# Output projection: a fifth pair by seven products in its first half, a pinned copy in the fold, and an add moved into the last matmul group

## The chip, the cores and the metric

The kernel runs on one core of one Trainium2 chip. The metric is device time in microseconds (us) of one execution, the median of several runs. Everything is one program of five engines that run side by side: PE (TensorE, matmuls; its weight loads are shown as PEld), DVE (VectorE), ACT (ScalarE), POOL (GpSimd) and SP (SyncE, which here only issues transfers), beside 16 DMA engines.

## The reference

One decoder block of width 2048 on 256 tokens, all in float32:

```python
proj = x @ w_in                       # columns: GLA q,k,v,gate,low rank; FoX q,k,v,f; two merge gates
y_gla = gla(...) @ w_branch_gla       # gated linear attention
y_fox = fox(...) @ w_branch_fox       # softmax attention with a forget bias
merged = sigmoid(ma) * y_gla + sigmoid(mb) * y_fox
x = layer_norm(ALPHA * x + merged @ w_out)
h = gelu(causal_dwconv(x @ w_gate)) * (x @ w_up)
x = layer_norm(ALPHA * x + h @ w_down)
x = x + sigmoid(x @ w_ple_gate) * (p @ w_ple_proj)
```

The change sits in `merged @ w_out` (the output projection, 256 x 2048 by 2048 x 2048), in the step that adds its partial sums into the residual, and at the very end of the last line.

## The kernel before

**Numbers as sums of two.** Matmuls run on a rounded format. Each float32 operand is split into a high part (a copy on ACT, line 121, tiles `hi`, `hi_b`, `hi_t`) and a low part (a subtraction on DVE, lines 215 and 241, tiles `lo`, `lo_b`, `lo_t`), and each product is three matmuls: high by high, high by low, low by high.

**Units.** All weights come from one array `wu` of 1 MB units, loaded by SP in program order (its schedule is written by hand, line 123), split by ACT and DVE, and used by PE. `unit(ahead=3)` (line 249) hands PE unit u and first prepares all up to u+2. Weights as loaded stand in the ring `raw` (5 buffers of half a unit), the split ones in `rhi` and `rlo` (6 buffers of half a unit each). The pool `big` (tag S8) has 15 buffers of 1 MB for all else that is large.

**Pairs and two ways to multiply them.** A projection with width 2048 runs in two halves of 1024 columns (`s_half`, line 818, `nh` 0 and 1). A unit holds the weights of one pair of 128 rows, as four 128 x 512 blocks: one pair by two column blocks; the activations of a pair are 2 x 2 blocks too (two row blocks by two token blocks). `classic` (line 844) does the eight block products, 24 matmuls of 128 x 512. `strassen` (line 852) does seven products of sums, 21 matmuls, whose results add up in seven PSUM accumulators. It needs sums of activation blocks (`mS`, made by `sums`, line 800) and differences of weight blocks (line 157). Which pairs go which way is in `WO_S`: pairs 1, 2, 3, 5 of the first half, 1, 3, 5 of the second. `OUT_ORDER` is the order of the pairs: 0, 1, 3, 4, 5, 2, 6, 7, and 0, 1, 3, 5, 2, 4, 6, 7. The output projection is units 120 to 135.

**Stored differences.** For the pairs in `WO_T` the weight differences are not made when they are needed but earlier, during the branch projections (units 96 to 119, the loop at line 1154): `park_gen` (line 174) loads a unit into an S8 buffer (line 178), lets two units of PE pass, makes the differences in place (four DVE operations of 128 x 512, line 159) and stores it with POOL's queue (line 172); each unit takes three of the 24 steps `pull(1, parks)` of that stage, so seven units take 21. When the pair's turn comes, `prep_s` (line 185) loads blocks b11 and b22, b21 from `wu` (lines 193 and 194; 0.25 and 0.5 MB) and the stored unit (line 196; 1 MB, into one more S8 buffer), and splits three and a half half-units instead of two.

**Activations.** `turn_pair` (line 1131) transposes one pair of the merged activations during the branch stage, pairs 6 and 7 in `begin_out` (line 1385) after the first unit. A pair in `WO_C` (0, 4, 6, 7) is split as it is into `mC`, two pairs to an S8 buffer; any other goes through `sums` into an S8 buffer of its own.

**Fold.** After the last seven-product pair of a half, `fold` (line 862) adds the accumulators p1, p5, p6, p7 into the residual tiles: one copy of p1 to SBUF on ACT (line 873) and eight DVE operations. DVE and ACT instructions are put in order when the program is built, by priority and by a simulation; `keep_in_program_order(i)` pins an instruction behind everything traced before it on its engine. Here the first DVE operation of the fold is pinned in first halves; the copy is not. `fold` serves four halves with a residual: two of the output projection and two of the down projection. The next half takes the accumulators' PSUM banks over.

**The end.** The last accumulator of the last half is made in two 256-column halves (line 906). For each, `ev_g` (line 1614) adds it on DVE to what is already summed in `zg` (line 1623), and `put` (line 1575) does tanh on ACT, two DVE operations and a store by SP.

Of the kernel before, what the change touches and what calls it, by code (L numbers as in the profile page):

```python
# [14 lines left out]
ALU = mybir.AluOpType  # L15
# [25 lines left out]
P_STAT = 5000  # L41
# [11 lines left out]
GR_T = ((1, 2, 5, 7), (1, 2, 5, 7))  # L53
GR_S = ((1, 2, 4, 5, 7),) * 2
X_S = (1, 2, 4, 5, 7)
WO_S = ((1, 2, 3, 5), (1, 3, 5))
WO_C = (0, 4, 6, 7)

DN_ORDER = (tuple(range(NF // 2)),
            tuple(range(NF // 2)))  # L60
DN_S = ((1, 3, 5, 6, 8, 9, 11, 12, 14, 15, 17, 18), (1, 3, 5, 6, 8, 9, 11, 12, 14, 15))


WO_T = ((1, 2, 3, 5), (1, 3, 5))
DN_T = ((3, 6, 9, 12, 15, 18), (3, 6, 9, 12, 15))
PG_ORDER = (tuple(range(8)), tuple(range(8)))
PG_S = ((), (2, 3, 4))
# [11 lines left out]
def tile_block(ctx: ExitStack, tc: tile.TileContext, wu, wfv, wpp, xT_in, x_in, pT_in, wlr,  # L79
               chan, gnorm, lng, ident_in, mask_in, cmask_in, out):  # L80
    nc = tc.nc
# [38 lines left out]
    def copy(o, i, scale=1.0):  # L120
        return nc.scalar.activation(o, i, AF.Copy, bias=0.0, scale=scale)  # L121
# [8 lines left out]
    for _ in range(8):  # L130
# [7 lines left out]
               for b, order, sset in ((52, GV_ORDER, GV_S), (68, GV_ORDER, GR_S),  # L138
                                      (120, OUT_ORDER, WO_S), (dn0, DN_ORDER, DN_S),
                                      (NU - 16, PG_ORDER, PG_S))  # L140
# [133 lines left out]
    ident = cst.tile([P, P], F32, name="ident")  # L274
# [183 lines left out]
    for u in range(8):  # L458
        hi, lo = fvu[u]
        for j in range(2):  # L460
# [8 lines left out]
            for t, i, c in seq:  # L469
# [3 lines left out]
                                 start=kt == 0 and i == 0, stop=kt == 15 and i == 2)  # L473
# [178 lines left out]
    for n in range(16):  # L652
        h, j = n // 2, n % 2
        hi, lo = unit()

        ps = (mxtile if n == 0 else mmtile)(f"psf{'qk'[j]}{h}")
# [112 lines left out]
    for n in range(16):  # L769
        nm, dst, sc = (("q", gq, 1.0 / 16.0), ("k", gk, 1.0))[n // 2 % 2]  # L770
        h, c = n // 4, n % 2
        hi, lo = unit()
        ps = mmtile(f"ps{nm}{2 * h + c}")
# [44 lines left out]
    def s_half(nm, nh, order, sset, cl, st, zof, ev, tail=0, mid={}, end=None, ahead=3,  # L818
               residual=True, fine=None):

        if nh == 0:
            C = [[mmtile(f"{nm}0_{t}{c}") for c in range(2)] for t in range(2)]
            p1, p5 = [mmtile(f"{nm}0_p{i}") for i in (1, 5)]
            p6 = p7 = None
        else:
            C = [[f(f"{nm}1_{t}{c}") for c in range(2)] for t, f in enumerate((mxtile, mmtile))]
            p1, p5, p6, p7 = [mmtile(f"{nm}1_p{i}") for i in (1, 5, 6, 7)]  # L830
        left = (0, 1, 6, 3, 5, 4, 2)
        n, ns = len(order), len(sset)
        total = {id(C[t][c]): 6 * (n - ns) + 3 * ns * (t * c == 0) for t in range(2)
                 for c in range(2)}
        if fine:
            total[id(C[1][1])] -= 6 * tail
        done = {}

        def mm(ps, x, w, e=slice(0, 512)):
            k = done[id(ps)] = done.get(id(ps), 0) + 1  # L840
            nc.tensor.matmul(ps[:, e], lhsT=x, rhs=w, start=k == 1,  # L841
                             stop=k == total.get(id(ps), 3 * ns))

        def classic(pair, w, toks=(0, 1), cs=(0, 1)):
            for j in range(2):
                for t in toks:
                    ah, al = cl(pair, j, t)
                    for x, v in ((ah, w[0][j]), (ah, w[1][j]), (al, w[0][j])):
                        for c in cs:
                            mm(C[t][c], x, v[:, c * 512:c * 512 + 512])  # L850

        def strassen(pair, ops):
            nonlocal p6, p7
            if p6 is None:
                p6, p7 = [mxtile(f"{nm}0_p{i}") for i in (6, 7)]
            prods = (p1, C[0][0], C[0][1], p5, p7, p6, C[1][0])
            for ps, i, (hi, lo) in zip(prods, left, ops):
                ah, al = st(pair, i)
                for x, v in ((ah, hi), (ah, lo), (al, hi)):
                    mm(ps, x, v)  # L860

        def fold():
            g0, g1 = 2 * nh, 2 * nh + 1
            u = t2("fold")
            axpy = lambda z, p: nc.vector.scalar_tensor_tensor(z, z, ALPHA, p, ALU.mult, ALU.add)
            add = lambda z, p: nc.vector.tensor_tensor(z, z, p, ALU.add)
            if not residual:
                copy(zof(0, g0), p1)
                for o, x, p in ((u, zof(0, g0), p6), (zof(0, g1), u, p5), (zof(1, g0), u, p7),
                                (zof(1, g1), zof(1, g0), p5)):  # L870
                    nc.vector.tensor_tensor(o, x, p, ALU.add)
                return
            copy(u, p1)
            i = axpy(zof(0, g0), p1)
            if nh == 0:
                tc.keep_in_program_order(i)
            add(u, p6)
            axpy(zof(0, g1), u)
            add(zof(0, g1), p5)
            add(u, p7)  # L880
            axpy(zof(1, g0), u)
            add(u, p5)
            axpy(zof(1, g1), u)

        for i, pair in enumerate(order[:n - tail]):
            (strassen if pair in sset else classic)(pair, unit())
            if i in mid:
                mid[i]()
            if pair in sset and not set(order[i + 1:]) & set(sset):
                fold()  # L890
        us = [unit(ahead) for _ in range(tail)]

        def tail_mm(t, c, i):
            classic(order[n - tail + i], us[i], (t,), (c,))
            if i == tail - 1:
                ev(t, c, C[t][c])

        if fine:
            fine(C[1][1])
            for t, c in ((0, 0), (0, 1), (1, 0)):  # L900
                for i in range(tail):
                    tail_mm(t, c, i)
            last = [(x, v[:, 512:1024]) for i in range(tail) for j in range(2)
                    for ah, al in (cl(order[n - tail + i], j, 1),)
                    for x, v in ((ah, us[i][0][j]), (ah, us[i][1][j]), (al, us[i][0][j]))]
            halves = [mmtile(f"{nm}{nh}_11{b}")[:, 0:256] for b in "bc"]
            for b, ps in enumerate(halves):
                for k, (x, v) in enumerate(last):
                    nc.tensor.matmul(ps, lhsT=x, rhs=v[:, 256 * b:256 * b + 256], start=k == 0,
                                     stop=k == len(last) - 1)  # L910
            ev(1, 1, None, halves)
            return
        if tail:
            end(tail_mm)
            return
        for t in range(2):
            for c in range(2):
                ev(t, c, C[t][c])
# [212 lines left out]
    def turn_pair(pair):  # L1131
# [7 lines left out]
        p3 = pt.rearrange("p (k t) -> p k t", t=S)  # L1139
        if pair not in WO_C:  # L1140
            yp = t2("yp")
            copy(yp, pt)
            mS[pair] = sums(yp.rearrange("p (k t) -> p k t", t=S), f"mS{pair}", 0.5,
                            pair not in WO_S[1])
            return
        i = WO_C.index(pair)
        if i % 2 == 0:
# [84 lines left out]
    def out_proj(nh, tail, mid, end=None):  # L1232
        def cl(pair, j, t):
            if pair not in WO_C:
                return cell(mS[pair], ((0, 7), (1, 2))[j][t])
            i = WO_C.index(pair)
            a = mC[i // 2][:, i % 2 * 2 + j, :]
            return a[:, t * P:t * P + P], a[:, 256 + t * P:256 + t * P + P]

        def ev(t, c, ps):  # L1240
            zc = z1of(t, 2 * nh + c)
            with tc.high_priority(P_STAT):
# [3 lines left out]

        s_half("wo", nh, OUT_ORDER[nh], WO_S[nh], cl, lambda pair, i: cell(mS[pair], i), z1of, ev,
               tail, mid, end)
# [160 lines left out]
    for n in range(NF):  # L1409
# [18 lines left out]
        u = t1("up")  # L1428
# [4 lines left out]
        if pair in DN_S[0]:  # L1433
            if j == 0:
                yp = t2("yp").rearrange("p (k t) -> p k t", t=S)
            h = yp[:, j, :]
        else:
            h = y
# [4 lines left out]
        if pair in DN_S[0] and j == 1:  # L1443
            v = s_sums(yp)
            for i in range(2):
# [4 lines left out]
                k = DN_S[0].index(pair)  # L1450
# [124 lines left out]
    def put(z, nh, t, c, ab=(0, 512)):  # L1575
        th = t2("tho")
        r = t2("res")
        e = slice(*ab)
        w = slice(c * 512 + ab[0], c * 512 + ab[1])
        o = slice(nh * 1024 + w.start, nh * 1024 + w.stop)  # L1580
        nc.scalar.activation(th[:, e], z, AF.Tanh, bias=0.0, scale=0.5)
        nc.vector.scalar_tensor_tensor(th[:, e], th[:, e], 1.0, pp[nh][:, t, w],
                                       ALU.add, ALU.mult)
        nc.vector.scalar_tensor_tensor(r[:, e], th[:, e], 0.5, z2[nh][:, t, w],
                                       ALU.mult, ALU.add)
        (nc.gpsimd if nh == 0 else nc.sync).dma_start(out[t, :, o], r[:, e])
# [27 lines left out]
    def ev_g(t, c, ps, halves=None):  # L1614
        z = zg[:, t, c, :]
        if halves is None:
            nc.vector.tensor_tensor(z, z, ps, ALU.add)
            put(z, 1, t, c)
            return
        for b, h in enumerate(halves):  # L1620
            e = slice(256 * b, 256 * b + 256)
            with tc.high_priority(P_STAT):
                nc.vector.tensor_tensor(z[:, e], z[:, e], h, ALU.add)
            put(z[:, e], 1, t, c, (e.start, e.stop))

    def pre_g(ps):
        z = zg[:, 1, 1, :]
# [61 lines left out]
def _layout(i):  # L1689
# [9 lines left out]
         _sst(c("gv", 2048), GV_ORDER, GV_S), _sst(c("gr", 2048), GV_ORDER, GR_S), m[PSM1:]] + br  # L1699
        + [_sst(i["w_out"][0], OUT_ORDER, WO_S), gu,  # L1700
           _sst(i["w_down"][0], DN_ORDER, DN_S),
# [44 lines left out]
```

## Time and profile before

| | |
|---|---|
| three runs | 1648.08, 1648.25, 1648.61 us; median 1648.25 |
| profiled execution, its own time | 1648.3 us |
| its span, first instruction to last | 1646.5 us |
| granted TensorE clock | 1.00 |
| busy: PE, PEld, DVE, ACT, POOL | 1639.6, 1405.6, 1339.6, 904.5, 89.5 us |
| DMA | 460.23 MB, mean 280 GB/s |

The profiled execution is one run; 1.8 us of its time lie outside the span (1648.3 less 1646.5). In rows of a timeline the columns are start, duration, engine, line, operation, tiles written and read, and the count of merged instructions; in brackets is the idle time ahead of it and what ended it. Durations of matmuls overlap their successors, so the pace of PE is read from the starts. Rows of stretches give start and end, length, then busy time and count of each engine, the granted clock, the DMA engines' busy share and GB/s. A wait is who waited, for whom, us in total, times, longest.

### The profile page before, as it was taken

The page shows a single profiled execution, that of the slowest core. Times are in us where ns is not written, and L with a number is a line of the kernel's source. Part 1 is how long each engine was busy: PE and PEld are TensorE (multiplying, and loading weights), DVE is VectorE, ACT ScalarE, POOL GpSimd, SP SyncE. Part 2 cuts the span into 40 slices and gives each one's busy share as a digit, 9 for nine tenths or more (in the row PEclk, how much of TensorE's full clock was granted, in tenths as well). Part 3 has the DMA queues.
Part 4 walks back from the last instruction along what each step waited for, and adds up shares of the span by engine and source line. Part 5 has one row for each costly group of instructions (what it writes and reads, how often), then busy time and mean ns, then how long its engine had stood idle before and what let it go on. Part 6 is the DMA issues. An engine that isn't in the chain of part 4 may idle for free.

```text
span 1646.5 us, 23416 instructions
## 1 busy us (share of the span) xinstructions
PE 1639.6 (100%) x8432; PEld 1405.6 (85%) x8432; DVE 1339.6 (81%) x1926; ACT 904.5 (55%) x1261; POOL 89.5 (5%) x238
## 2 busy tenths in 40 slices
PE   9999999999999999999999999999999999999998
PEld 8988888888888888888898888888888888888887
DVE  7677789898889767777987888887877778989787
ACT  6655545456666654446574444555555456566554
POOL 0000000000000000000010111110111000000000
PEclk9999999999999999999999999999999999999999
DMA  8777689977887658888855898888766679899574
GB/s 323 279 261 278 230 322 344 373 269 281 298 292 268 227 197 309 306 309 316 299 191 190 314 341 319 302 306 306 282 237 216 210 260 339 306 353 340 169 260 157
DMA packets 112100, 460.23 MB, mean 280 GB/s; under 512 B 12728, under 2 KB 14016, under 8 KB 94704
## 3 DMA queue, kind: packets, MB, share of 16 engines
q1 hardware_dynamic: 103344, 406.30, 69.3%
q0 software_dynamic: 8640, 52.44, 8.1%
q8 instruction: 66, 1.08, 0.3%
q14 instruction: 50, 0.41, 0.1%
HBM read 406.25 MB, written 52.44 MB: 279 GB/s over the span
## 4 chain that ended last, share of the span: by engine, by line
PE 98%; DMA 1%; DVE 0%; ACT 0%; issue 0%; POOL 0%; SPq 0%; DVEq 0%; ACTq 0%; POOLq 0%
PE psm L973 11%; PE dn L841 10%; PE psu L307 10%; PE psg L307 9%; PE psa L973 5%; PE psu L309 5%; PE psg L309 5%; PE dn_p L841 4%; PE gv L841 3%; PE gr L841 3%; PE wo L841 3%; PE pg L353 3%; PE psb L973 3%; PE fv L472 2%; PE psk L307 2%; PE psq L307 2%
## 5 line engine op out<-in xcount | busy, mean ns | idle before, releaser
L241 DVE TENSOR_TENSOR lo<-raw,hi 128x1024 fp32r<-128x1024 f32 x464 | 561.4, 1220 | 165.9 <-ACT hi L121 163.9
L121 ACT ACTIVATE hi<-raw 128x1024 fp32r<-128x1024 f32 x464 | 486.5, 1058 | 342.8 <-issue 66.2
L307 PE MATMUL psu<-x1T,hi 128*128 128x512 f32 x688 | 240.4, 392 | 0.0
L307 PE MATMUL psg<-x1T,hi 128*128 128x512 f32 x672 | 234.8, 392 | 0.0
L309 PE MATMUL psu<-x1T,lo 128*128 128x256 f32 x688 | 192.3, 280 | 0.0
L309 PE MATMUL psg<-x1T,lo 128*128 128x256 f32 x672 | 187.8, 280 | 0.0
L973 PE MATMUL psm<-hi,xT 128*128 128x512 f32 x512 | 162.9, 392 | 0.0
L307 PEld LDWEIGHTS psu<-x1T,hi 128*128 128x128 f32 x688 | 129.1, 188 | 27.6
L307 PEld LDWEIGHTS psg<-x1T,hi 128*128 128x128 f32 x672 | 126.1, 188 | 27.0
L309 PEld LDWEIGHTS psu<-x1T,lo 128*128 128x128 f32 x688 | 130.6, 190 | 0.0
L121 ACT ACTIVATE hi_b<-raw 128x512 fp32r<-128x512 f32 x104 | 87.1, 842 | 77.2 <-issue 20.8
L309 PEld LDWEIGHTS psg<-x1T,lo 128*128 128x128 f32 x672 | 127.6, 190 | 0.0
L215 DVE TENSOR_TENSOR lo_b<-raw,hi_b 128x512 fp32r<-128x512 f32 x104 | 98.4, 954 | 33.0 <-ACT hi_b L121 32.6
L973 PEld LDWEIGHTS psm<-hi,xT 128*128 128x128 f32 x512 | 96.2, 188 | 19.6
L159 DVE TENSOR_TENSOR td<-td 128x512 f32<-128x512 f32 x148 | 101.2, 684 | 0.6
L973 PE MATMUL psm<-lo,xT 128*128 128x512 f32 x256 | 99.7, 390 | 0.0
L841 PE MATMUL dn<-hi,hC 128*128 128x512 f32 x352 | 97.8, 389 | 0.0
L215 DVE TENSOR_TENSOR lo_t<-td,hi_t 128x1024 fp32r<-128x1024 f32 x74 | 87.6, 1218 | 8.4 <-ACT hi_t L121 7.6
L121 ACT ACTIVATE hi_t<-td 128x1024 fp32r<-128x1024 f32 x74 | 77.1, 1055 | 19.3 <-DMA td<-td 3.8
L973 PE MATMUL psa<-hi,oT 128*128 128x512 f32 x256 | 81.2, 392 | 0.0
L841 PEld LDWEIGHTS dn<-hi,hC 128*128 128x128 f32 x352 | 66.0, 188 | 13.7
L121 ACT ACTIVATE hi_t<-raw 128x1024 fp32r<-128x1024 f32 x30 | 31.9, 1062 | 45.6 <-DVE raw L159 38.2
(412 smaller groups left out, 3144.9 us busy)
## 6 DMA issues: line engine op xcount, KB each, us to landing
raw<-in_wu_dram SPq DMA_DIRECT2D x531, 512.0 KB, 5.8
td<-in_wu_dram SPq DMA_DIRECT2D x37, 1024.0 KB, 8.5
td<-td POOLq DMA_DIRECT2D x37, 1024.0 KB, 6.1
td<-td SPq DMA_DIRECT2D x37, 1024.0 KB, 7.7
hS<-sd SPq DMA_DIRECT2D x11, 1024.0 KB, 8.3
raw<-in_wu_dram SPq DMA_DIRECT2D x37, 256.0 KB, 6.2
fvraw<-in_wfv_dram SPq DMA_DIRECT2D x13, 524.0 KB, 6.7
sd<-hs POOLq DMA_DIRECT2D x24, 256.0 KB, 5.6
```

What stands on the lines that cost most here:

```text
L121: return nc.scalar.activation(o, i, AF.Copy, bias=0.0, scale=scale)
L159: sub = lambda o, a, b: nc.vector.tensor_tensor(o, a, b, ALU.subtract)
L215: nc.vector.tensor_tensor(lo, src, hi.bitcast(F32), ALU.subtract)
L241: i = nc.vector.tensor_tensor(lo, raw, hi.bitcast(F32), ALU.subtract)
L307: nc.tensor.matmul(ps, lhsT=hi[i // 8 if hoff == 0 else 0][:, w0 % 1024:w0 % 1024 + P], rhs=a[:, kt % 4, :], start=first and i == 0, stop= ...
L309: nc.tensor.matmul(ps[:, 256:512], lhsT=lo[i // 8 if hoff == 0 else 0][:, w0 % 1024:w0 % 1024 + P], rhs=a[:, kt % 4, 0:256], start=False, ...
L353: nc.tensor.matmul(bs[j][:, 0:m], lhsT=x, rhs=v[:, o:o + m], start=first and i == 0, stop=last and i == 2)
L472: nc.tensor.matmul(fbk[t][c][:, 0:n], lhsT=x, rhs=w[:, o:o + n], start=kt == 0 and i == 0, stop=kt == 15 and i == 2)
L841: nc.tensor.matmul(ps[:, e], lhsT=x, rhs=w, start=k == 1, stop=k == total.get(id(ps), 3 * ns))
L973: nc.tensor.matmul(ps[t], lhsT=x, rhs=v, start=first and i == 0 and j == 0, stop=last and i == 3 and j == 2)
```

## The change

Three edits. Pair 4 of the first half of the output projection goes from `classic` to `strassen` (`WO_S`), with its differences stored beforehand (`WO_T`), so that eight units are stored in the branch stage, and it leaves `WO_C`: its activations are kept as eight blocks by `sums`, and pairs 0 and 6 now share one `mC` buffer while 7 has the second. The copy of p1 in the fold is pinned in program order, in all four halves with a residual. And for the last 256 columns of the kernel the sum so far is added by one more matmul, identity by `zg`, in the middle of the last accumulation group, in place of the DVE add; `put` then reads PSUM.

```diff
-WO_S = ((1, 2, 3, 5), (1, 3, 5))
-WO_C = (0, 4, 6, 7)
+WO_S = ((1, 2, 3, 4, 5), (1, 3, 5))
+WO_C = (0, 6, 7)
...
-WO_T = ((1, 2, 3, 5), (1, 3, 5))
+WO_T = ((1, 2, 3, 4, 5), (1, 3, 5))
...
-            copy(u, p1)
+            tc.keep_in_program_order(copy(u, p1))
             i = axpy(zof(0, g0), p1)
...
                 for k, (x, v) in enumerate(last):
                     nc.tensor.matmul(ps, lhsT=x, rhs=v[:, 256 * b:256 * b + 256], start=k == 0,
                                      stop=k == len(last) - 1)
+                    if b and k == len(last) // 2:
+                        nc.tensor.matmul(ps, lhsT=ident, rhs=zof(1, 3)[:, 256:512], start=False,
+                                         stop=False)
...
             e = slice(256 * b, 256 * b + 256)
-            with tc.high_priority(P_STAT):
-                nc.vector.tensor_tensor(z[:, e], z[:, e], h, ALU.add)
-            put(z[:, e], 1, t, c, (e.start, e.stop))
+            if b == 0:
+                with tc.high_priority(P_STAT):
+                    nc.vector.tensor_tensor(z[:, e], z[:, e], h, ALU.add)
+            put(h if b else z[:, e], 1, t, c, (e.start, e.stop))
```

## The prediction

> **What bounds the kernel now.** First the page's head, its busy line and the chain that ended last.
>
> ```profile
> span 1646.5 us, 23416 instructions
> PE 1639.6 (100%) x8432; PEld 1405.6 (85%) x8432; DVE 1339.6 (81%) x1926; ACT 904.5 (55%) x1261; POOL 89.5 (5%) x238
> PE 98%; DMA 1%; DVE 0%; ACT 0%; issue 0%; POOL 0%; SPq 0%; DVEq 0%; ACTq 0%; POOLq 0%
> ```
>
> PE is busy for all but 6.9 us and is 98% of the chain, so an edit is worth what it does to PE's matmul count, to PE's waits, or to what follows the last matmul. The waits of PE come next; ahead of them stands pair 0 of the output projection, for the pace.
>
> ```profile
> 739.89 0.62 PE L841 MATMUL wo<-hi,mC 128*128 128x512 f32 x2
> 745.34 1.03 PE L1137 MATMUL mt<-ident,sg 128*128 128x128 f32 x8
> 746.13 0.48 PE L841 MATMUL wo_p<-hi_b,mS 128*128 128x512 f32 x1
> ...
> PE wo_p L841 <- ACT hi_t L121: 0.5, 2, 0.3
> ```
>
> Its 24 matmuls take 745.34 - 739.89 = 5.45 us, 0.227 us each; a seven-product pair of 21 takes 4.76. Beside the first matmuls of the program, the only wait of PE is the last row, in this very stage. Its place is pair 2, the last seven-product pair of the first half:
>
> ```profile
> 765.95 0.39 PE L841 MATMUL wo_p<-hi_b,mS 128*128 128x512 f32 x1
> ...
> 767.76 0.39 PE L841 MATMUL wo<-hi_b,mS 128*128 128x512 f32 x1
> 768.42 0.73 PE L841 MATMUL wo_p<-hi_t,mS 128*128 128x512 f32 x2 [0.27 <-ACT hi_t L121]
> 769.37 0.50 PE L841 MATMUL wo_p<-hi_t,mS 128*128 128x512 f32 x1 [0.21 <-ACT hi_t L121]
> 769.71 0.39 PE L841 MATMUL wo<-hi_t,mS 128*128 128x512 f32 x1
> ```
>
> By the starts, four matmuls take 769.71 - 767.76 = 1.95 us instead of 0.91: 1.04 us lost (the idle marks show half, since a matmul's end overlaps the next). Why `hi_t` was late stands in ACT's timeline, SP's issue of the stored unit (with its own DMA row: size, us to landing) and ACT's wait:
>
> ```profile
> 761.39 1.06 ACT L121 ACTIVATE hi_b<-raw 128x1024 fp32r<-128x1024 f32 x1 [1.35 <-PE wo L841]
> 766.83 0.60 ACT L121 ACTIVATE fold<-wo_p 128x512 f32<-128x512 f32 x1 [4.38 <-PE wo_p L841]
> 767.32 1.99 ACT L121 ACTIVATE hi_t<-td 128x1024 fp32r<-128x1024 f32 x2
> ...
> 755.50 0.42 SPq L196 DMA_DIRECT2D td<-td  x1
> td<-td SPq DMA_DIRECT2D x1, 1024.0 KB, 6.9
> ...
> ACT fold L121 <- PE wo_p L841: 4.5, 2, 4.4
> ```
>
> The stored unit had landed at 755.50 + 6.9 = 762.4. But ACT's order has the fold's copy of p1 ahead of the two `hi_t`, and p1 is complete only inside pair 2: ACT stood still for 4.38 us in front of a copy that nobody needed yet.
>
> **The change part by part.** *Pair 4 by seven products:* 24 matmuls become 21, 3 x 0.227 = **-0.68 us** on PE, if its operands are there.
>
> *The pinned copy:* it now stands behind all copies traced before it, those of pairs 2, 6 and 7. The `hi_t` of pair 2 can then run from 762.4 on, and the **-1.04 us** come back if the landing allows it. What is late next is the copy: pair 7's second copy needs a buffer that pair 2 frees with its ninth matmul, at 765.27 (765.95 less 0.68) + 2.04 = 767.3; one copy of 1.06 later the fold's runs at 768.4 instead of 766.83. In the down projection I cost it at nothing: the only waits of such a copy in the whole trace are the two of the last row, both on `wo_p`; and three plain pairs (3 x 5.45 us) follow the fold of its first half, six that of its second, before anything takes the banks. Without that cover a copy pushed back by two or three splits costs PE up to 3 us.
>
> *The added work off PE.* The eighth store adds four differences on DVE, 4 x 0.68 = 2.7 us. The sums of pair 4 add four additions of 0.28 and four subtractions for the one there was, some 2.1 us of DVE and 1.7 of ACT. Pair 4's unit splits half a unit and a quarter more: 0.95 + 3 x 1.18 (2.35 for two, below) in place of 2 x 1.18, 2.1 us of DVE, and about as much of ACT.
>
> ```profile
> L159 DVE TENSOR_TENSOR td<-td 128x512 f32<-128x512 f32 x148 | 101.2, 684 | 0.6
> L797 DVE TENSOR_TENSOR sums<-yp x8: 281/283/285, 658.3 to 725.7; 128x128 f32<-128x128 f32 x8
> L215 DVE TENSOR_TENSOR lo_b<-raw,hi_b 128x512 fp32r<-128x512 f32 x104 | 98.4, 954 | 33.0 <-ACT hi_b L121 32.6
> 610.00:740.00 130.00, 130.00 (x586) 107.55 (x585) 94.69 (x128) 56.62 (x66) 3.79 (x7) 1.00 0.84 305
> 764.00:768.00 4.00, 4.00 (x19) 3.10 (x17) 0.00 (x0) 1.17 (x2) 0.00 (x0) 1.00 1.03 426
> 788.00:794.00 6.00, 6.00 (x29) 4.95 (x28) 6.00 (x8) 4.66 (x5) 0.00 (x0) 1.00 0.91 311
> 787.30 2.35 DVE L215 TENSOR_TENSOR lo_t<-td,hi_t 128x1024 fp32r<-128x1024 f32 x2
> 788.09 0.39 PE L841 MATMUL wo_p<-hi_b,mS 128*128 128x512 f32 x1
> ```
>
> The branch stage hides 4.8 us easily: DVE idles 35 of 130 us there. In the projection the cover is the very idle time that the misplaced copy made: DVE does nothing from 764 to 768. Later the cover is thin: from 788 on DVE is busy throughout, and the first `lo_t` of the second half is ready at 787.30 + 1.2 = 788.5, while PE wants it with the eleventh matmul of the pair, at 788.09 + 2.27 = 790.4. PE comes 1.7 us earlier now; DVE, no longer held until 768.4, comes some 2 us earlier. I take 0 for it, between 0 and 1.7 (PE waits for all it gained).
>
> *The added transfers.* The store is 1 MB more on POOL's queue and its load 1 MB more on SP's; pair 4's unit reads 0.25 + 0.5 + 1 instead of 1 MB. Stretches of the DMA engines:
>
> ```profile
> 718.00:724.00 6.00, 6.00 (x30) 4.92 (x30) 5.50 (x7) 2.67 (x4) 0.00 (x0) 1.00 0.39 134
> 736.00:742.00 6.00, 6.00 (x28) 4.95 (x28) 4.53 (x6) 2.12 (x2) 0.00 (x0) 1.00 1.02 431
> 748.00:752.00 4.00, 4.00 (x19) 3.30 (x19) 4.00 (x5) 3.40 (x4) 0.00 (x0) 1.00 0.86 336
> 752.00:756.00 4.00, 4.00 (x20) 3.30 (x19) 3.74 (x5) 2.95 (x5) 0.00 (x0) 1.00 0.65 212
> ```
>
> The load falls ahead of 724, where the DMA engines stand 61% idle. The store comes three units of 5.45 us after the seventh's (724.34, below), at 740.7, and falls with pair 4's 0.75 MB into a stretch that is full to 748 and again from 756. 1.75 MB (1.84 million bytes) at 431 GB/s are 4.3 us; 0.14 x 4 + 0.35 x 4 = 2.0 us of them fit into 748 to 756, so pair 2's stored unit lands 2.3 us later, at 764.7. Its first `hi_t` is then ready at 765.8 and `lo_t` at 767.0; PE wants them with the tenth and eleventh matmul, at 767.3 and 767.5. It just holds: 0 again, between 0 and 2.0 (if the two idle stretches can't be used).
>
> The Trainium skill ("DMA: Bandwidth & Descriptors", section Bandwidth) says that for transfers between HBM and SBUF the HBM side binds, at about 358 GB/s for a core. By that the extra bytes would take 5.1 us, 3.2 after the idle stretches, and PE would wait 0.7 us: the time of the forecast plus 0.7. The 431 GB/s above say that this core gets more, so the trace's rate stands.
>
> *The end:*
>
> ```profile
> 1641.35 0.28 PE L909 MATMUL pg_11c<-hi,x2T 128*128 128x256 f32 x1
> 1641.67 0.42 DVE L1623 TENSOR_TENSOR zg<-zg,pg_11c 128x256 f32<-128x256 f32 x1
> 1642.12 0.42 ACT L1581 ACTIVATE tho<-zg 128x256 f32<-128x256 f32 x1 [1.49 <-DVE zg L1623]
> 102.09 0.59 PE L628 MATMUL po<-pts,fv 128*128 128x256 f32 x2
> 102.53 0.38 PE L630 MATMUL po<-pts,fv 128*128 128x128 f32 x2
> ```
>
> Without the DVE add the tanh starts 1642.12 - 1641.67 = 0.45 us earlier. The new matmul has full float32 operands of 256 columns, as L628, which takes two records: 102.53 - 102.09 = 0.44 us on PE. Between -0.01 and, with 0.1 for changing formats, +0.1; I take +0.05.
>
> **Sum:** -0.68 - 1.04 + 0.05 = -1.67 us on the profiled execution (1648.3, span 1646.5, 1.8 outside it), and 1648.25 - 1.67 = **1646.6** for the median.
>
> **Rivals.** *B, the transfers are late.* DMA is full on both sides of the two idle stretches, and issues there wait for ring buffers, so the idle time may not be usable; then pair 2's unit lands 4.3 us later, at 766.7, and PE waits about 2 us where it waited 1.04: 1648.6. Against it: the 6.9 us to landing above contain queueing that a late issue would not have.
>
> *C, slower: SP is held by an S8 buffer.* Fifteen buffers; when SP wants the sixteenth it stands, and all later loads with it. When pair 4's stored unit is to be loaded (the third of its kind), there are two `z1`, five `mS` and one `mC`, `sg1` and `sg3`, one `ofTr`, the stored units of pairs 1 and 3, and the eighth unit on its way out: 14 or 15, where before there were 12. That the pool is already close shows here:
>
> ```profile
> 724.34 0.53 POOL L172 DMA_DIRECT2D td<-td  x1 [15.77 <-DVE td L159]
> td<-td POOLq DMA_DIRECT2D x1, 1024.0 KB, 10.6
> SPq L1300 <- DMA td<-td: 3.3, 1, 3.3
> td<-td SPq DMA_DIRECT2D x1, 1024.0 KB, 8.5
> ```
>
> The load of `z1` waited 3.3 us for the store of the seventh unit to land (10.6 us after its issue; the last row is the third load of a stored unit before, pair 5's). If pair 4's load is given the eighth's buffer, it goes out at 740.7 + 10.6 = 751.3 and lands 8.5 later at 759.8; `hi_t` is ready at 760.9, wanted with pair 4's tenth matmul at 746.13 + 2 x 4.76 + 2.04 = 757.7: 3.2 us of waiting, and by my estimate some 0.7 more at pair 2, whose loads queue behind. 1646.6 + 3.9 = 1650.5. It decides against the change as soon as SP is held beyond about 749; held so that all 7 us show, 1653.6. Against it: `ofTr`, `sg3` and pair 1's unit come free between 735 and 743, and any of them will do.
>
> *D, the fold takes over the wait.* The second half's first accumulators take the banks of p6 and p7, last read here:
>
> ```profile
> 777.62 0.67 DVE L866 TENSOR_TENSOR fold<-fold,wo_p 128x512 f32<-128x512 f32 x1
> ```
>
> done at 778.3; PE wants them at 788.09 - 5.45 - 1.72 = 780.9. If the chain shifts by the copy's 1.6 us it still holds by 1.0; with DVE's order made anew it may cost up to 1 us: 1647.6.
>
> **How the numbers follow.** Forecast 0.50 (its own range 1646.2 to 1647.3), B 0.20, C 0.17, D 0.08, and 0.05 for orders on ACT and DVE that come out otherwise somewhere else. Range 1646.0 to 1650.6: the forecast, B, D and half of C; left out are C's upper half and most of the rest. What a measurement here can tell from no change is about 0.2%, 3.3 us: below 1644.95 the gain would have to be twice the sum, 0.03; above 1651.55 lie C's upper part and some of the rest, 0.13; within, 0.84.
>
> **What would show it.** Right: no wait of PE on `hi_t` in pair 2; ACT's fold copy behind pair 7's second copy; 8431 matmul records (8432 - 3 + 2); PE's start of the second half's pair 1 near 786.4; tanh within 0.1 us of the last matmul. Wrong: SP idle at the load of pair 4's stored unit (C), ACT waiting for that of pair 2 past 766 (B), PE waiting on `fold` near 781 (D), or PE waiting on `lo_t` after 786.

## The result and the profile after

| | before | after |
|---|---|---|
| median of 22 runs each (range), us | 1648.64 (1648.05 to 1649.66) | 1646.66 (1645.80 to 1647.98) |
| profiled execution, its own time | 1648.3 | 1646.57 |
| its span | 1646.5 | 1644.8 |
| bytes moved by DMA | 460.23 MB | 463.12 MB |

The ratio of after to before is 0.9988, with a 95% interval of 0.9983 to 0.9994: 1.98 us faster, 1.0 to 2.8 by the interval. The forecast was 1646.6 us. Two lines from the head of the page of the changed kernel, and then all that its view of PE's waits lists:

```profile
span 1644.8 us, 23446 instructions
PE 1638.5 (100%) x8431; PEld 1405.9 (85%) x8431; DVE 1345.6 (82%) x1938; ACT 908.7 (55%) x1267; POOL 90.3 (5%) x239
...
PE warm_ps L131 <- DVE warm L128: 1.2, 1, 1.2
PE fv L472 <- ACT xT L121: 0.3, 1, 0.3
```

There are 8431 matmul records, one fewer than before, and the wait on `hi_t` is gone. The two rows left belong to the first matmuls of the program. The start of four pairs in PE's timeline (pairs 1, 4 and 2 of the first half, and pair 1 of the second) shows where the time came from:

```profile
746.10 0.48 PE L841 MATMUL wo_p<-hi_b,mS 128*128 128x512 f32 x1
...
755.72 0.39 PE L841 MATMUL wo_p<-hi_b,mS 128*128 128x512 f32 x1
...
765.24 0.39 PE L841 MATMUL wo_p<-hi_b,mS 128*128 128x512 f32 x1
...
786.32 0.39 PE L841 MATMUL wo_p<-hi_b,mS 128*128 128x512 f32 x1
```

Pair 1 starts at 746.10 (746.13 before), pair 2 at 765.24 (765.95), the second half's pair 1 at 786.32 (788.09). So 0.68 us came between pairs 1 and 2, where pair 4 lies, and 1.06 us (from 788.09 - 765.95 = 22.14 to 786.32 - 765.24 = 21.08) behind the start of pair 2, where the stall was. The rest of the program follows at this distance.

The inside of pair 2, in the timelines of PE, ACT and DVE:

```profile
767.28 0.84 PE L841 MATMUL wo_p<-hi_t,mS 128*128 128x512 f32 x3
...
768.19 0.39 PE L841 MATMUL wo_p<-lo_t,mS 128*128 128x512 f32 x1
...
764.91 2.01 ACT L121 ACTIVATE hi_t<-td 128x1024 fp32r<-128x1024 f32 x2 [1.45 <-DMA td<-td]
766.83 3.17 ACT L121 ACTIVATE hi<-raw 128x1024 fp32r<-128x1024 f32 x3
770.41 1.06 ACT L121 ACTIVATE hi<-raw 128x1024 fp32r<-128x1024 f32 x1 [0.41 <-PE wo L841]
771.37 0.58 ACT L121 ACTIVATE fold<-wo_p 128x512 f32<-128x512 f32 x1
...
766.01 2.36 DVE L215 TENSOR_TENSOR lo_t<-td,hi_t 128x1024 fp32r<-128x1024 f32 x2 [0.66 <-ACT hi_t L121]
```

ACT's 1.45 us ahead of `hi_t` are now a wait for the transfer and no longer 4.38 us behind a copy that nobody needed. Three readers can come too late. The first `hi_t`, ready at 764.91 + 1.06 = 765.97, is read by the tenth matmul at 767.28: 1.3 us to spare. The second `hi_t`, ready at 764.91 + 2.01 = 766.92, is read by the twelfth at 767.28 + 2 x 0.227 = 767.73: 0.8 us. (That the twelfth reads it shows in the stall of before: ACT finished the second copy at 767.32 + 1.99 = 769.31, and the twelfth matmul started at 769.37.) The first `lo_t`, ready at 766.01 + 2.36 / 2 = 767.2, is read by the fourteenth at 768.19: about 0.95 us. So the slack of pair 2 is 0.8 us, and it is the second `hi_t` that will be late first.

### The profile page after: what moved, and what is told of

Same layout as the page of the kernel before. It is cut to its first block, busy times and chain, and to the rows that moved or that the text cites. A ratio compares the mean times of both kernels' runs of the same rounds, so it can differ in the third digit from the quotient of the medians.

```text
span 1644.8 us, 23446 instructions
## 1 busy us (share of the span) xinstructions
PE 1638.5 (100%) x8431; PEld 1405.9 (85%) x8431; DVE 1345.6 (82%) x1938; ACT 908.7 (55%) x1267; POOL 90.3 (5%) x239
## 2 busy tenths in 40 slices
DMA packets 112533, 463.12 MB, mean 282 GB/s; under 512 B 12776, under 2 KB 14064, under 8 KB 94752
## 4 chain that ended last, share of the span: by engine, by line
PE 99%; DMA 0%; ACT 0%; DVE 0%; POOL 0%; issue 0%; SPq 0%; POOLq 0%
PE psm L976 11%; PE dn L841 10%; PE psu L307 10%; PE psg L307 9%; PE psa L976 5%; PE psu L309 5%; PE psg L309 5%; PE dn_p L841 4%; PE wo L841 3%; PE gv L841 3%; PE gr L841 3%; PE pg L353 3%; PE psb L976 3%; PE fv L472 2%; PE psk L307 2%; PE psq L307 2%
## 5 line engine op out<-in xcount | busy, mean ns | idle before, releaser
L241 DVE TENSOR_TENSOR lo<-raw,hi 128x1024 fp32r<-128x1024 f32 x462 | 559.8, 1222 | 164.3 <-ACT hi L121 161.9
L976 PE MATMUL psm<-hi,xT 128*128 128x512 f32 x512 | 163.0, 392 | 0.0
L976 PEld LDWEIGHTS psm<-hi,xT 128*128 128x128 f32 x512 | 96.2, 188 | 19.6
L976 PE MATMUL psm<-lo,xT 128*128 128x512 f32 x256 | 99.8, 390 | 0.0
L841 PE MATMUL dn<-hi,hC 128*128 128x512 f32 x352 | 97.9, 389 | 0.0
L976 PE MATMUL psa<-hi,oT 128*128 128x512 f32 x256 | 81.2, 392 | 0.0
L841 PEld LDWEIGHTS dn<-hi,hC 128*128 128x128 f32 x352 | 66.0, 188 | 13.6
```

Source lines behind the costliest of these rows:

```text
L241: i = nc.vector.tensor_tensor(lo, raw, hi.bitcast(F32), ALU.subtract)
L841: nc.tensor.matmul(ps[:, e], lhsT=x, rhs=w, start=k == 1, stop=k == total.get(id(ps), 3 * ns))
L976: nc.tensor.matmul(ps[t], lhsT=x, rhs=v, start=first and i == 0 and j == 0, stop=last and i == 3 and j == 2)
```

## The experiments

The median of the kernel before differs a little from one set of runs to the next (1648.64 to 1648.94); each ratio is against runs of the kernel before on the same chip at the same time. Effects of 1 us are near what a ratio can tell, so every verdict rests on PE's starts in the trace as well. "Lost" means here: PE's first to last start in a stretch, less 0.227 us for each matmul in it; for the stall of before that gives 1.06 us.

### The parts one at a time

Four kernels made from the one before: the pin alone, pair 4 alone, the end alone, and the first two together.

```diff
# pin alone
-            copy(u, p1)
+            tc.keep_in_program_order(copy(u, p1))
# pair 4 alone
+WO_S = ((1, 2, 3, 4, 5), (1, 3, 5))
+WO_C = (0, 6, 7)
+WO_T = ((1, 2, 3, 4, 5), (1, 3, 5))
```

> Only the copy of p1 in the fold is pinned. The forecast's theory (the stall in pair 2 comes from this copy standing ahead of the stored half's copies): the 1.04 us lost between the sixth and the tenth matmul of pair 2 are gone, time 1.0 us below before. Rival (the stored half was late by its transfer anyway, or the fold takes over the wait): less than 0.4 us gained, with PE waiting in pair 2 or at the start of the second half.

> Only pair 4 goes by seven products, with the eighth store; the copy is not pinned and the end is as before. The forecast's theory: 0.68 us gained on the matmuls and the stall in pair 2 as large as before (about 1 us) or larger, since the pair's stored half lands at 764.8 and the fold's copy still stands ahead of it; time 0.7 us below before. Rival (the longer row of seven-product pairs moves the copy's place by itself): the stall is gone without the pin, 1.7 us below before. Rival (the extra transfers cost time): not faster than before.

> Only the add in the last matmul group. Theory: it costs PE 0.43 to 0.54 us and saves 0.45 to 0.5 between the last matmul and the tanh; time within 0.15 us of before. Rival (the new matmul costs only what a high-part matmul of 256 columns does, 0.12 us): 0.35 us faster. Rival (it breaks up the group): over 0.3 us slower.

> The changed kernel with the end of before. Theory: the first two edits make the whole gain, 1.7 us below before and within 0.15 us of the changed kernel. Rival (the end edit carries part of it): 0.3 us or more slower than the changed kernel.

| kernel | median, us (range) | against before, us | ratio, 95% interval | span |
|---|---|---|---|---|
| pin alone | 1647.54 (1647.30 to 1648.31) | -1.20 | 0.9994, 0.9985 to 1.0003 | 1645.2 |
| pair 4 alone | 1647.92 (1647.78 to 1648.28) | -0.82 | 0.9995, 0.9986 to 1.0004 | 1646.2 |
| end alone | 1648.44 (1647.99 to 1649.45) | -0.30 | 0.9999, 0.9990 to 1.0008 | 1647.4 |
| pin and pair 4 | 1646.87 (1646.68 to 1647.80) | -1.87 | 0.9990, 0.9981 to 0.9999 | 1645.1 |

The differences of medians add up (1.20 + 0.82 = 2.02, together 1.87), though only the last interval of the table excludes no change. What was expected of the end alone and of the two edits together is finer than these times can tell. What the trace shows is sharper. ACT and PE with the pin alone, then with pair 4 alone:

```profile
762.42 2.01 ACT L121 ACTIVATE hi_t<-td 128x1024 fp32r<-128x1024 f32 x2 [0.22 <-DMA td<-td]
...
767.51 0.39 PE L841 MATMUL wo<-hi_b,mS 128*128 128x512 f32 x1
767.74 0.84 PE L841 MATMUL wo_p<-hi_t,mS 128*128 128x512 f32 x3
```

```profile
766.24 0.60 ACT L121 ACTIVATE fold<-wo_p 128x512 f32<-128x512 f32 x1 [2.57 <-PE wo_p L841]
766.73 1.99 ACT L121 ACTIVATE hi_t<-td 128x1024 fp32r<-128x1024 f32 x2
...
767.17 0.39 PE L841 MATMUL wo<-hi_b,mS 128*128 128x512 f32 x1
767.83 0.73 PE L841 MATMUL wo_p<-hi_t,mS 128*128 128x512 f32 x2 [0.27 <-ACT hi_t L121]
...
769.11 0.39 PE L841 MATMUL wo<-hi_t,mS 128*128 128x512 f32 x1
```

With the pin, ACT copies the stored half as soon as it has landed, and PE goes on at its pace (0.23 us from 767.51 to 767.74). Without it, pair 4 alone, the fold's copy again stands ahead of the two `hi_t`, and PE loses the same: 769.11 - 767.17 = 1.94 us for four matmuls, 1.03 over the 0.91 of their pace. So the stall comes from ACT's order and not from the transfers, and pair 4's 0.68 us do not depend on it. With the pin and pair 4 together PE has no wait in pair 2.

### Is the eighth store worth its transfers

The changed kernel with pair 4's differences made when they are needed, not stored:

```diff
-WO_T = ((1, 2, 3, 4, 5), (1, 3, 5))
+WO_T = ((1, 2, 3, 5), (1, 3, 5))
```

> The changed kernel, but pair 4's weight differences are made when they are needed and not stored beforehand. That takes 1 MB of store, 1 MB of load and 0.75 MB of reads away and moves four differences of 0.6 to 0.7 us on DVE from the branch stage into a stretch (748 to 772) where DVE has about 2 us of idle time. Theory (the store pays by keeping DVE free): PE waits 0.3 to 1.5 us for pair 4's or pair 2's stored halves, 0.3 to 1.5 us slower than the changed kernel. Rival (the store is not needed, DVE's 2 us and the freed transfers cover it): no wait of PE, within 0.2 us of the changed kernel.

Measured: 1649.52 us (1648.29 to 1650.83), ratio 1.0004 (0.9995 to 1.0013): 2.9 us above the changed kernel by the medians, twice the upper end of what was expected. The profiled execution is its fastest (1648.29, span 1646.3). PE's waits there, ACT's copies of pair 4's made halves, and DVE ahead of pair 2's low part:

```profile
PE wo_p L841 <- DVE lo_b L215: 0.6, 1, 0.6
PE wo L841 <- DVE lo_b L215: 0.4, 1, 0.4
...
753.27 1.06 ACT L121 ACTIVATE hi_t<-raw 128x1024 fp32r<-128x1024 f32 x1 [1.24 <-DVE raw L159]
757.04 1.06 ACT L121 ACTIVATE hi_t<-raw 128x1024 fp32r<-128x1024 f32 x1 [2.70 <-DVE raw L159]
...
765.55 0.75 DVE L1283 TENSOR_TENSOR pTs<-pTr,pTs 128x256 fp32r<-128x256 f32 x2
766.22 1.82 DVE L215 TENSOR_TENSOR lo_b<-raw,hi_b 128x512 fp32r<-128x512 f32 x2
```

The four differences sit in DVE's queue between the splits: ACT waits 1.24 and 2.70 us for them, DVE then works through a backlog without a break from 758.13 to 768, and `lo_b` of pair 2, wanted at about 765.3, is only begun at 766.22. PE loses 2.0 us there, on the low part of pair 2's first pieces and not, as was expected, on stored halves; the profiled executions differ by 1.7 (1648.29 against 1646.57). The other 1.2 us of the medians are not in this trace, and where the slower runs lose them stays open.

### How thin is pair 2's slack

A needless copy from DRAM to DRAM is put ahead of pair 2's loads, of 0.25, 0.5 or 1 MB (n = 512, 1024, 2048) in the changed kernel, and of 1 MB in the kernel with the pin alone.

```diff
+    xd = dr.tile([P, n], F32, name="xd")
...
+        if u == 125:
+            nc.sync.dma_start(xd, wu[0, :, 0:n])
```

> The same with 0.25 MB. Theory: 0.6 to 1.2 us more of transfers against 0.3 to 0.5 us to spare: PE waits 0.1 to 0.9 us around pair 2. Rival: no wait.

> The changed kernel with a needless copy of 0.5 MB ahead of the loads of pair 2. Theory (a slack of 0.95 us, from the first low part's end at 767.24 to the matmul that reads it at 768.19, after which each us of lateness is paid): 0.5 MB moves the landing by half of the 3.3 us that 1 MB moved it, 1.2 to 1.65 us, and TensorE waits 0.2 to 0.7 us in pair 2, a time of 1646.8 to 1647.5. Rival (the wait grows in proportion to the bytes): half of the 2.43 us of 1 MB, 1.2 us, a time near 1647.9.

> The changed kernel with one needless copy of 1 MB between two DRAM buffers, issued by SP just ahead of pair 2's loads. Theory (pair 2's stored half just holds, with 0.3 to 0.5 us to spare between the first low part on DVE and the matmul that reads it): 1 MB takes 2.5 us of full transfer engines, or up to twice that as it reads and writes the same memory, so PE waits 2 to 4.5 us around pair 2 and the time is as much above the changed kernel. Rival (the transfers have several us in hand there): PE waits less than 0.5 us.

> The kernel before with the pinned fold copy alone, and a needless copy of 1 MB from DRAM to DRAM ahead of the loads of pair 2. Theory: without pair 4's stored half the half of pair 2 lands at about 762.3 instead of 764.7 us, so that the first matmul that reads its low part has some 3.4 us of slack instead of 0.95; a copy of 1 MB, which moved the landing by 3.3 us in the changed kernel, then costs TensorE at most 0.3 us in pair 2, and the time stays within 0.4 us of the pin alone (1647.5). Rival (pair 2's slack was as thin before pair 4 was changed): 2 us or more of waiting in pair 2, a time near 1649.8.

| kernel | median, us (range) | ratio, 95% interval | PE lost in pair 2 |
|---|---|---|---|
| changed, 0.25 MB | 1646.79 (1646.09 to 1648.44) | 0.9989, 0.9980 to 0.9998 | 0 |
| changed, 0.5 MB | 1647.45 (1646.72 to 1649.64) | 0.9991, 0.9982 to 1.0001 | 0.6 |
| changed, 1 MB | 1648.91 (1648.41 to 1650.13) | 1.0002, 0.9993 to 1.0011 | 2.6 |
| pin alone, 1 MB | 1647.96 (1647.55 to 1648.97) | 0.9996, 0.9987 to 1.0006 | 0 |

PE's rows at the `hi_t` of pair 2, with 0.5 MB and with 1 MB, then ACT's and PE's with the pin alone and 1 MB (in these kernels lines stand three further down, L844 for L841):

```profile
766.99 0.67 PE L844 MATMUL wo_p<-hi_t,mS 128*128 128x512 f32 x2
767.88 0.50 PE L844 MATMUL wo_p<-hi_t,mS 128*128 128x512 f32 x1 [0.21 <-ACT hi_t L121]
```

```profile
766.44 0.73 PE L844 MATMUL wo<-hi_b,mS 128*128 128x512 f32 x2 [0.25 <-ACT hi_b L121]
767.70 0.50 PE L844 MATMUL wo<-lo_b,mS 128*128 128x512 f32 x1 [0.53 <-DVE lo_b L218]
...
770.16 0.50 PE L844 MATMUL wo_p<-hi_t,mS 128*128 128x512 f32 x1 [0.22 <-ACT hi_t L121]
```

```profile
765.88 2.01 ACT L121 ACTIVATE hi_t<-td 128x1024 fp32r<-128x1024 f32 x2 [1.38 <-DMA td<-td]
...
768.29 0.84 PE L844 MATMUL wo_p<-hi_t,mS 128*128 128x512 f32 x3
```

A dose that fits the slack costs nothing (0.25 MB: the theory of that run took the slack for 0.3 to 0.5 us and missed; its rival held). One a little beyond it costs 0.6 us, and the wait is that of the twelfth matmul for the second `hi_t`, as the slack of 0.8 us says; the expectation had `lo_t` late first. 1 MB also delays the two pieces that are loaded ahead of the stored one (`hi_b`, `lo_b`), so that PE pays more than once. The wait is a threshold and not in proportion to the bytes.

With the pin alone the same 1 MB costs PE nothing. Without it, the second `hi_t` is ready at 762.42 + 2.01 = 764.43 and read at 767.74 + 0.45 = 768.19 (the fence of the pin alone), 3.8 us to spare; with it, at 767.89 against 768.74, 0.85 us are left. Its median is 0.4 us above that of the pin alone (0.2 when each is taken against the kernel before of its own runs), yet PE's only wait beyond the start's usual one is another of 0.7 us, early in the program (`fv` on ACT's `fvhi`, L475), far from the copy. So pair 4 is cheaper by 0.68 us, and pair 2's slack shrinks from 3.8 to 0.8 us.

### One pair more

The changed kernel with pair 6 by seven products too, its differences made on the spot:

```diff
-WO_S = ((1, 2, 3, 4, 5), (1, 3, 5))
-WO_C = (0, 6, 7)
+WO_S = ((1, 2, 3, 4, 5, 6), (1, 3, 5))
+WO_C = (0, 7)
```

> The changed kernel with pair 6 of the first half by seven products too (differences made on the spot, its sums kept as eight blocks, pairs 0 and 7 in one buffer). 0.68 us less of matmuls again, but the fold then has one plain pair (5.45 us) ahead of the second half instead of two. Theory (the cover of the fold is what the pin lives on): the copy of p1 runs after 775, p7 is read about 4.8 us later, at 780 to 781, and the second half wants its bank at about 780.2: PE waits 0.5 to 2.5 us there, time between the changed kernel's and 2 us above it. Rival (the fold moves up with its pair): no wait, 0.7 us below the changed kernel.

Measured: 1650.97 us (1649.94 to 1651.86), ratio 1.0011 (1.0002 to 1.0020): 4.3 us above the changed kernel, beyond both expectations. Its waits of PE, and busy time by stretch (columns: length, then busy time and count of PE, PEld, DVE, ACT, POOL; granted clock; DMA's share; GB/s):

```profile
PE wo_p L841 <- ACT hi_t L121: 1.3, 2, 0.7
...
PE wo L841 <- DVE lo L241: 1.2, 2, 1.0
PE wo_p L841 <- DVE lo_t L215: 0.7, 1, 0.7
...
756.00:764.00 8.00, 8.00 (x37) 6.64 (x36) 8.00 (x10) 6.65 (x10) 0.00 (x0) 1.00 0.94 343
772.00:780.00 8.00, 6.71 (x27) 4.93 (x28) 7.68 (x8) 5.99 (x7) 0.00 (x0) 1.00 0.54 182
```

No wait is on a PSUM bank or on `fold`, which was my theory; it fell. The fold read p7 until 785.5 us there, some 4 us after PE would want its bank by the forecast's way of reckoning (the second half's pair 1 starts at 788.49; less 5.45 and 1.72 that is 781.3), and PE did not wait: either it wants the bank later than was thought, or its order of matmuls came out otherwise; no run here tells which. DVE is busy for 8.00 and 7.68 us of these two stretches of 8, and PE waits for what comes out of that queue, up to the last half's plain pairs (`lo`, L241, at 816 us). One of these waits goes by way of a transfer: `lo_t` at 801 us was late because ACT had waited 2.3 us for a stored unit, whose load SP issued only at 791.92, as an earlier `lo_t` of DVE ended (791.90). Three matmuls fewer save 0.68 us and bring four differences, more splits and more sums into a stretch where DVE has no room; PE loses 2.8 us from 766 to 777 and 2.7 from 799 to 820.

## Why the prediction held, step by step

**Pair 4.** -0.68 us predicted; -0.68 by PE's starts, -0.82 by the medians of pair 4 alone.

**The pinned copy.** -1.04 predicted; 1.06 by the starts, 1.20 by the medians of the pin alone. What was put too early is the copy itself: 768.4 predicted, 771.37 measured. The step let it wait for a buffer of pair 2 and one copy. In fact the `hi_t` themselves came only at 764.91, three copies (3.17 us from 766.83) follow them, and the fourth waited another 0.41 us, until 770.41. By that time pair 2's ninth matmul, which frees the buffer by the forecast, was long done (767.4); what came just then was the fourth's own load (issued at about 764.2, 6.1 us to landing: 770.3), and the run of the pin and pair 4 marks the same wait as one for that load. The late copy cost nothing, since the fold's last read of p7 still came early:

```profile
775.47 0.68 DVE L866 TENSOR_TENSOR fold<-fold,wo_p 128x512 f32<-128x512 f32 x1
```

It ends at 776.15, 2.1 us earlier than before, and PE wants that bank, by the forecast's estimate, at 780.9 - 1.7 = 779.2. That is rival D's place, and by this estimate it has 3 us of room; the experiment with a sixth pair, where PE did not wait, speaks for more. The pinned copies of the down projection cost nothing either: PE's list of waits has no row from there.

**The transfers.** Landing of pair 2's stored half: 764.7 predicted, 757.35 + 7.5 = 764.85 measured. The time came out right, but partly by luck, since the way there was another. It is read from these rows of SP, of POOL, of the transfers issued there, and of the DMA engines' stretches:

```profile
757.35 0.33 SPq L196 DMA_DIRECT2D td<-td  x1
td<-td SPq DMA_DIRECT2D x1, 1024.0 KB, 7.5
...
746.79 0.53 POOL L172 DMA_DIRECT2D td<-td  x1 [19.38 <-DVE td L159]
td<-td POOLq DMA_DIRECT2D x1, 1024.0 KB, 10.5
...
748.00:752.00 4.00, 4.00 (x19) 3.32 (x18) 3.90 (x5) 2.98 (x4) 0.00 (x0) 1.00 1.00 322
752.00:756.00 4.00, 4.00 (x20) 3.30 (x19) 3.75 (x4) 2.95 (x5) 0.00 (x0) 1.00 1.00 419
764.00:768.00 4.00, 4.00 (x20) 3.30 (x19) 3.34 (x4) 3.09 (x4) 0.00 (x0) 1.00 1.01 401
```

The forecast let the load go out at its old time (755.50) and take 2.3 us longer on full DMA engines. In fact it took 0.6 us longer (7.5 against 6.9) and went out 1.85 us later. SP's last wait ahead of it was one of 0.6 us for a transfer of `td` (the second row of SP's waits below), and the times say which: the eighth store landed at 746.79 + 10.5 = 757.29, the load went out at 757.35. So it waited for the S8 buffer that the store still held. In five other profiled executions (pair 4 alone, the pin and pair 4, and the three doses of the changed kernel) the load also goes out within 0.1 us of the store's landing, at 756.7 to 758.4 us; with a sixth pair SP came to it later anyway. The store's landing thus sets much of the slack: with the pin and pair 4 it came at 758.34, and the slack of pair 2 was 0.5 us.

The two idle stretches (0.86 and 0.65 busy before) are full now by their share, but only the second moves more bytes (212 GB/s before, 419 now; the first 336 and 322). Rival B, which doubted that the idle time could be used, did not occur at its size, though its reason, loads that are issued late, did. Three things on the way were off. The eighth store went out at 746.79, not 740.7 (its four differences wait in DVE's queue until 746.5). The spare time was 0.8 us, not the 0.5 of the forecast, which had `lo_t` read by the eleventh matmul of the pair where it is read by the fourteenth, and did not cost the second `hi_t`. And two prices leave out that spare time: by the forecast's own figures a landing at 765.6 makes PE wait 0.4 us, not 0.7, and rival B's at 766.7 1.4 us, not 2. The doses confirm the slack: with 0.25 MB no wait, with 0.5 MB 0.6 us.

The rule of the Trainium skill that spoke against the change ("DMA: Bandwidth & Descriptors", section Bandwidth: the HBM side binds at about 358 GB/s) would have put the landing 0.9 us later, at 765.6. The landing cannot judge it, as most of the delay lies ahead of the issue; the rates can, and the trace does not agree: 419 and 401 GB/s in the last two rows. Its page "HBM Reference", section Specifications, fits better: a core that streams alone gets well above its share of a shared domain, about 425 GB/s.

**DVE.** Costed at nothing, up to 1.7 us: it is nothing. In place of the idle 764 to 768 DVE is busy for 3.34 of 4 us there, and the experiment without the store and the one with a sixth pair show what happens when four differences more (with the sixth pair, more splits and sums too) fall into this stage: 2.0 and 5.5 us of PE's time lost.

**SP and the sixteenth buffer.** Rival C occurred in small, at two loads. Two rows of SP's waits between 600 and 860 us, the issue of pair 4's stored load in SP's timeline, and its transfer:

```profile
SPq L196 <- PE psb L976: 4.1, 2, 3.7
...
SPq L196 <- DMA td<-td: 0.6, 1, 0.6
...
740.06 0.33 SPq L196 DMA_DIRECT2D td<-td  x1
td<-td SPq DMA_DIRECT2D x1, 1024.0 KB, 9.0
```

SP stood 3.7 us for an S8 buffer at pair 4's load, as feared. It was one that the branch stage's last matmuls (into `psb`, L976) free, and not the eighth store's, which was the one that held pair 2's load (the second row): pair 4's load went out at 740.06 and landed at 749.1, where the rival needed a hold beyond about 749. Pair 4 wants the stored half with its tenth matmul, at 755.72 + 2.04 = 757.8, 8.7 us after the landing.

**The end.** +0.05 predicted, some -0.08 measured. PE's, then ACT's rows there:

```profile
1638.75 0.59 PE L912 MATMUL pg_11c<-zg,ident 128*128 128x256 f32 x2
1638.99 0.47 PE L909 MATMUL pg_11c<-lo,x2T 128*128 128x256 f32 x1
1639.29 0.40 PE L909 MATMUL pg_11c<-hi,x2T 128*128 128x256 f32 x2
...
1640.01 0.28 PE L909 MATMUL pg_11c<-hi,x2T 128*128 128x256 f32 x1
1640.32 0.38 ACT L1584 ACTIVATE tho<-pg_11c 128x256 f32<-128x256 f32 x1 [1.45 <-PE pg_11c L909]
```

From 1638.75 to 1639.29 lie 0.54 us, of which one product of the group is 0.12: the added matmul costs 0.42. From the last matmul's start to the tanh are 0.31 us instead of 0.77, and the tanh takes 0.38 instead of 0.42: 0.42 - 0.46 - 0.04. The 0.42 are near the 0.44 of L628, so no loss for changing formats, for which the forecast allowed 0.1 us, shows on top of them. The end alone measured -0.30, with an interval of -1.6 to +1.3 us; it cannot be told from nothing by the time.

**The sum.** -1.67 predicted, -1.73 in the profiled execution (1646.57 against 1648.3), -1.98 by the medians. The two large terms are right in their mechanism; that the terms put at nothing stayed at nothing hung on 0.8 us of slack, which was not reckoned at the right place.

## What to carry to other kernels

Where PE is 98% of the path, read first what waits ahead of a late operand on its own engine: here a copy that nobody needed yet held a needed one for 4.4 us, and giving it a later place was worth more than the matmuls saved. A unit by seven products is worth its 0.68 us only if its extra differences and transfers fall into time that is idle; measure that room in microseconds at every reader and go by the smallest, since a wait starts only beyond it (none at 0.25 MB, 2.6 us at 1 MB). Ask of each added transfer what buffer it holds and who waits for that: here the eighth store held up pair 2's load, though the two have no data in common. And a slack that one edit leaves is what the next edit spends: the fifth pair fitted with 0.8 us to spare, the sixth did not.

## What was not expected

The unstored variant's median lies 1.2 us above the time of its profiled execution, its fastest, and its runs spread over 2.5 us; all other medians agree with their profiled execution within some 1.0 us either way. No trace here shows where the slower runs lose it. Part of all scatter is in the first 20 us of the program, where the wait of `fv` is 0.3 us in one profiled execution and 0.8 in another (end alone) with the same code. And a full share of the DMA engines is not one rate: the stretches from 748 to 752 and from 752 to 756 us both have a share of 1.00, the first at 322 GB/s and the second at 419, with the eighth store on its way in both. The store need not be the cause: before the change, with no such store, 756 to 760 us has a share of 1.00 at 325 GB/s. The share tells when there is no room left, not how much was moved.
